# Ordering page loads and page work behind a dense tile's own, and holding the FFN's tiles open over the second out-projection, in a two-layer decoder step

## Chip, cores and metric

One core of one Trainium2 chip runs the whole program. The metric is the device time of one execution in microseconds (us), given as the median of several runs. A profiled execution of the same kernel gives the trace.

## What is computed

The reference runs two layers of a hybrid decoder on 1024 prompt tokens and, with the same weights, on 8 sample tokens that attend to 1024 past tokens in a paged cache. For this case the second part of each layer matters: the sample tokens' attention over the cache, the output projection, and the gated FFN.

```python
# sample tokens: pages of the cache, softmax over past and new keys, difference of two maps
k_past = cache_k[l, page_table].reshape(DB, -1, DIFF_HEADS, 2, DIFF_DK)
v_past = cache_v[l, page_table].reshape(DB, -1, DIFF_HEADS, DIFF_DV)
od = diff_attn_sample(q, k, v, k_past, v_past, lam)
og, s_new = gla_chunk(state_gla[l].astype(jnp.float32), gq, gk, gv, glog)
# both groups of tokens
def merge(o_diff, o_gla, gate, subln_l, gla_norm_l, lam_init, w_out_l):
    od = rmsnorm(o_diff, subln_l) * (1.0 - lam_init)
    og = rmsnorm(o_gla, gla_norm_l).reshape(B, T, GLA_HEADS * GLA_DV) * jax.nn.silu(gate)
    o = jnp.concatenate([od.reshape(B, T, DIFF_HEADS * DIFF_DV), og], axis=-1)
    return o @ w_out_l
def ffn(h, norm2_l, w_gu_l, w_down_l):
    n = rmsnorm(h, norm2_l)
    a, b = jnp.split(n @ w_gu_l, 2, axis=-1)
    return (jax.nn.silu(a) * b) @ w_down_l
```

Everything is float32, D_MODEL is 1024 and D_FF is 2816.

## The kernel before

A layer has three stages. The first two (`phase_d` and `phase_g`) make the input projection, the prompt's attention and the gated linear attention. The third, which the change is about, is the dense stage with the cache work of the sample tokens beside it.

**Dense stage.** The tokens are split in two halves: half 0 has 512 columns, half 1 has 512 and the 8 sample tokens. A half runs `out_half` (out-projection, 8 weight tiles) and then `ffn_half`. The FFN's 22 blocks of 128 come in chunks of 4, the last of 2. A chunk has `gates` (4 weight tiles), `ups` (4) and `down` (8 tiles of 4 blocks each, 2 in the last chunk). The order is gates(0), then for each chunk ups(c), gates(c+1), down(c). Half 0 works in pairs of tiles that share one accumulation group `psd`.

Each weight tile goes through `prep_tile`: SyncE (SP) loads `raw` (3 buffers), ScalarE rounds it to `wh` (3 buffers), VectorE subtracts to get the rest `wl` (2 buffers), each in pieces of 4 blocks (128x512). `gemm3` then issues three matmuls for every block: `wh` with the activations' high part, `wh` with their low part, `wl` with the high part. So SP, ScalarE and VectorE all work ahead of TensorE, by at most 3, 3 and 2 tiles.

`out_half` reads two inputs: `oHa`, `oLa` (attention, loaded from scratch memory by SP) and `oHb`, `oLb` (split on ScalarE and VectorE from `og`, which is on chip), and contracts the a part first. After a group the residual is added, and `new_x` makes the new `xH` and `xL`.

**Cache work.** `decode` reads 64 pages of keys and 64 pages of values (256 KB each, 5 buffers of tag `page`). A key page is multiplied with the query on GpSimd (`page<-page,qbd`) and reduced on VectorE (`sall<-page`). Then comes a softmax, and each value page is weighted either on ScalarE and added on GpSimd, or weighted and added on VectorE (`vacc`). `sample_gla` does the sample tokens' linear attention on GpSimd. All of this runs beside half 0; half 1 needs its result `osf`.

**What sets the order.** A clock written into the code: `dense(us)` and `mix(us)` set the priority of what is traced next to a place on a common clock and move on, by 5.6 us for a gate or up tile and by 1.8 or 1.6 us for a key or value page, times `MIX_RATE` 1.4. The scheduler takes, on each engine, the instruction of the smallest clock value among those that it holds for ready. Each engine then runs its list in order, SP's queue of loads too. `load_page` reads the page's number and issues the load, with an order kept only to the fourth page load before.

**Memory.** Tile pools are stacked; the pool `op` of the second out-projection stands where the pool `fp` of the first FFN half stood, and so waits until that has been read for the last time.

Of the kernel before, what the change touches and what calls it, by code (L numbers as in the profile page):

```python
# [21 lines left out]
P = 128  # L22
# [4 lines left out]
NB = 8  # L27
# [7 lines left out]
MIX_RATE = 1.4  # L35
# [8 lines left out]
NPB = 5  # L44
# [13 lines left out]
def f(ap):  # L58
    return ap.bitcast(F32)
# [3 lines left out]
def hybrid_kernel(  # L63
# [26 lines left out]
    clock = {"base": 0, "top": 0, "dense": 0.0, "mix": 0.0, "rate": 1.0}  # L90

    def span_start():
        clock.update(base=tc.cur_priority + 10, top=0, dense=0.0, mix=0.0)

# [8 lines left out]
    def mix(us):  # L103
        at(clock["mix"])
        clock["mix"] += us * clock["rate"]
# [18 lines left out]
    def tt(out, a, b, op, eng=None):  # L124
        (eng or DVE).tensor_tensor(out, a, b, op=op)  # L125
# [129 lines left out]
    def layer(l):  # L255
# [7 lines left out]
        with ExitStack() as octx:  # L263
# [12 lines left out]
            with ExitStack() as pctx:  # L276
# [17 lines left out]

    def load_page(dst, src, idx):
        with ExitStack() as st:
            if len(page_dma) >= 4:
                st.enter_context(tc.issue_after(page_dma[-4].ins))
            r = SP.value_load(pt_sb[0:1, idx:idx + 1], min_val=0, max_val=NPHYS - 1)
        page_dma.append(SP.dma_start(dst, src[bass.ds(r, 1)].rearrange("o p c -> (o p) c")))  # L300
# [581 lines left out]
    def prep_tile(wps, src, nk):  # L882
        raw = wps[0].tile([P, KD, P], F32, name="raw", tag="raw", bufs=3)
        SP.dma_start(raw[:, :nk, :], src.rearrange("(k p) c -> p k c", p=P))
# [56 lines left out]
    def out_half(l, X, og, osf, ac, wps, psD):  # L941
        W = COLS[X]
        acc = ac.tile([P, KD, WM], F32, name="acc", tag="acc")
        with ExitStack() as st:
# [16 lines left out]
            for js in groups(X, list(range(KD))):  # L961
                ps = psD.tile([P, 2, 512], F32, name="psd", tag="d")
                ws = []
                for half in range(2):
                    for u, j in enumerate(js):
# [3 lines left out]
                        gemm3(unit_outs(ps, X, u), *ws[u], ah, al, range(half * H, half * H + H), first=half == 0, last=half == 1)  # L969
# [9 lines left out]
    def ffn_half(l, X, acc, ac, wps, psD, psn):  # L979
# [3 lines left out]
        with ExitStack() as st:  # L983
            fp = st.enter_context(tc.tile_pool(name="fp", bufs=1, reuse_waits="tile"))
            xh = lambda k: xH[:, k, t0:t0 + W]
            xl = lambda k: xL[:, k, t0:t0 + W]
            chunks = [list(range(c, min(c + 4, NF))) for c in range(0, NF, 4)]
            r = rstd[:, t0:t0 + W].unsqueeze(1)

            def gates(c):  # L990
                sa = fp.tile([P, 4, WM], F32, name="sa", tag="sa", bufs=1)
                for fs in groups(X, chunks[c]):
                    ps = psD.tile([P, 2, 512], F32, name="psd", tag="d")
                    for u, ff in enumerate(fs):
                        dense(5.6)
                        ws = prep_tile(wps, w_gu[l, :, ff * P:(ff + 1) * P], KD)
                        gemm3(unit_outs(ps, X, u), *ws, xh, xl, range(KD))
                    if fs[0] == 0:
                        rms_half(X, psn)
                    n = len(fs)  # L1000
                    i0 = fs[0] - chunks[c][0]
                    tt(unit_view(sa[:, i0:i0 + n, :W], X, n), unit_ps(ps, X, n),
                       unit_view(bc(r, [P, n, W]), X, n), ALU.mult)
                n = len(chunks[c])
                last_silu.append(act(sa[:, :n, :W], sa[:, :n, :W], AF.Silu))
                if X == 0 or c == len(chunks) - 1:
                    load_ln_exp()
                return sa

            def ups(c, sa):  # L1010
                hs = []
                for fs in groups(X, chunks[c]):
                    ps = psD.tile([P, 2, 512], F32, name="psd", tag="d")
                    for u, ff in enumerate(fs):
                        dense(5.6)
                        ws = prep_tile(wps, w_gu[l, :, DFF + ff * P:DFF + (ff + 1) * P], KD)
                        gemm3(unit_outs(ps, X, u), *ws, xh, xl, range(KD))
                    n = len(fs)
                    i0 = fs[0] - chunks[c][0]
                    g = 2 if X == 0 else 1  # L1020
                    tb = fp.tile([P, g, W], F32, name="tb", tag="tb", bufs=1)[:, :n, :]
                    tt(unit_view(tb, X, n), unit_ps(ps, X, n), unit_view(bc(r, [P, n, W]), X, n), ALU.mult)
                    tt(tb, tb, sa[:, i0:i0 + n, :W], ALU.mult)
                    hh = fp.tile([P, g, W], F32R, name="hh", tag="hh", bufs=6 // g)[:, :n, :]
# [283 lines left out]
```

## Time and profile before

| What | Value |
|---|---|
| Median of 3 runs | 2929.18 us (2924.52 to 2933.24) |
| Profiled execution | 2921.56 us, its span 2919.8 us |
| TensorE matmul busy | 2738.3 us (94%) |
| VectorE busy | 1801.9 us (62%) |
| ScalarE busy | 1359.9 us (47%) |
| GpSimd busy | 386.8 us (13%) |
[...]
| SP's queue of loads | 290.90 MB, 33.9% of 16 DMA engines |

The dense stage of the first layer runs from about 534 us to 1460 us of the span, that of the second from about 1975 us to the end, half 0 first (to about 1020 and 2463 us). Busy shares are means over stages with different limits; what an edit in one stage is worth has to be read there. A line such as "[5.14 <-DVE wl]" gives the idle time of an engine ahead of an instruction, and what ended it.

### The profile page before, as it was taken

What the parts mean: (1) busy time and instruction counts of PE and PEld (TensorE: products, weight loads), DVE (VectorE), ACT (ScalarE), POOL (GpSimd) and SP (SyncE); (2) the same over time, 40 slices, a digit from 0 to 9 for tenths busy, and PEclk for the clock granted to TensorE, in tenths of its full rate; (3) what the DMA queues carried; (4) which work ended last, traced back from release to release, by engine and by line L of the source; (5) the groups of instructions that cost most, each with busy time, mean ns of one, the idle gap of its engine ahead of it and who ended that gap; (6) DMA issues with size and microseconds to landing.
All of it is one profiled execution on the core that took longest, in us unless ns stands there. A gap on an engine that the chain in (4) does not pass through costs nothing.

```text
span 2919.8 us, 46807 instructions
## 1 busy us (share of the span) xinstructions
PE 2738.3 (94%) x16906; PEld 2420.4 (83%) x16906; DVE 1801.9 (62%) x3549; ACT 1359.9 (47%) x3343; POOL 386.8 (13%) x333
## 2 busy tenths in 40 slices
PE   8999899969999899999999989999699997999999
PEld 7887787757778699999988868887577885999998
DVE  6777577567775564444577766675778743544444
ACT  7888445423543343222378874454235432322222
POOL 1000000076230000000010000000943300000000
PEclk9999999989999999999999999999799998999999
DMA  4121111267673252332221111113767624223322
GB/s 129 58 58 38 46 31 44 86 198 224 203 205 105 76 151 84 97 95 87 66 50 57 40 33 55 49 45 115 218 187 220 186 81 134 87 88 94 94 85 83
DMA packets 461322, 298.13 MB, mean 102 GB/s; under 512 B 34698, under 2 KB 416906, under 8 KB 461090
## 3 DMA queue, kind: packets, MB, share of 16 engines
q1 hardware_dynamic: 452322, 290.90, 33.9%
q10 hardware_dynamic: 8704, 4.20, 0.5%
q8 instruction: 134, 2.20, 0.3%
q14 instruction: 98, 0.80, 0.1%
q0 software_dynamic: 64, 0.03, 0.0%
HBM read 271.53 MB, written 23.53 MB: 101 GB/s over the span
## 4 chain that ended last, share of the span: by engine, by line
PE 73%; DVE 10%; ACT 8%; DMA 3%; issue 3%; POOL 2%; SPq 1%; DVEq 0%; ACTq 0%; POOLq 0%
PE psd L82 52%; PE psq L82 4%; PE psqk L82 3%; PE psv L82 3%; PE psgg L82 2%; PE po L82 2%; ACT sc L88 2%; ACT qn L88 1%; PE psS L82 1%; POOL page L125 1%; ACT qhh L88 1%; DVE wl L125 1%; PE tpw L85 1%; PE poG L82 1%; DVE gA L720 1%
## 5 line engine op out<-in xcount | busy, mean ns | idle before, releaser
L88 ACT ACTIVATE wh<-raw 128x512 fp32r<-128x512 f32 (+1 forms) x608 | 353.1, 614 | 946.6 <-PE psd L82 753.1
L82 PE MATMUL psd<-xH,wh 128*128 128x260 f32 (+1 forms) x2112 | 681.5, 323 | 39.3 <-ACT wh L88 39.3
L82 PE MATMUL psd<-xH,wl 128*128 128x260 f32 (+1 forms) x2112 | 683.4, 324 | 14.1 <-DVE wl L125 14.0
L82 PE MATMUL psd<-xL,wh 128*128 128x260 f32 (+1 forms) x2112 | 679.1, 322 | 0.6 <-DVE xL L128 0.6
L125 DVE TENSOR_TENSOR wl<-raw,wh 128x512 fp32r<-128x512 f32 (+1 forms) x608 | 444.5, 748 | 108.0 <-issue 57.6
L82 PEld LDWEIGHTS psd<-xH,wh 128*128 128x128 f32 x2112 | 400.0, 189 | 71.1 <-ACT wh L88 40.2
L82 PEld LDWEIGHTS psd<-xH,wl 128*128 128x128 f32 x2112 | 400.2, 190 | 50.8 <-DVE wl L125 18.8
L82 PEld LDWEIGHTS psd<-xL,wh 128*128 128x128 f32 x2112 | 400.3, 190 | 33.8 <-DVE xL L128 1.8
L82 PE MATMUL psd<-hh,wl 128*128 128x260 f32 (+1 forms) x1056 | 341.8, 324 | 12.9 <-DVE wl L125 12.8
L82 PE MATMUL psd<-hh,wh 128*128 128x260 f32 (+1 forms) x1056 | 341.4, 324 | 9.9 <-ACT hh L88 8.6
L82 PE MATMUL psd<-hl,wh 128*128 128x260 f32 (+1 forms) x1056 | 339.8, 322 | 0.3 <-DVE hl L125 0.2
L125 DVE TENSOR_TENSOR acc<-psd,acc 128x520 f32<-128x520 f32 (+1 forms) x144 | 125.7, 873 | 169.6 <-PE psd L82 169.6
L82 PEld LDWEIGHTS psd<-hh,wl 128*128 128x128 f32 x1056 | 200.6, 190 | 33.4 <-DVE wl L125 19.0
L82 PEld LDWEIGHTS psd<-hh,wh 128*128 128x128 f32 x1056 | 200.6, 190 | 25.9 <-ACT hh L88 9.7
L82 PEld LDWEIGHTS psd<-hl,wh 128*128 128x128 f32 x1056 | 200.5, 190 | 16.1 <-DVE hl L125 2.0
L125 POOL TENSOR_TENSOR page<-page,qbd 128x512 f32<-128x512 f32 x128 | 185.9, 1484 | 45.6 <-DMA page<-in_cache_k 37.1
L82 PE MATMUL psq<-wh,xH 128*128 128x384 f32 (+1 forms) x512 | 180.4, 352 | 7.6 <-DVE zs L125 4.7
L82 PE MATMUL psq<-wh,xL 128*128 128x384 f32 (+1 forms) x512 | 179.9, 352 | 0.0
L82 PE MATMUL psq<-wl,xH 128*128 128x384 f32 (+1 forms) x512 | 179.3, 350 | 0.0
L125 DVE TENSOR_TENSOR sa<-psd,rstd 128x520 f32<-128x520 f32 (+1 forms) x66 | 57.6, 873 | 184.7 <-PE psd L82 180.6
L125 DVE TENSOR_TENSOR tb<-psd,rstd 128x520 f32<-128x520 f32 (+1 forms) x66 | 57.6, 872 | 152.2 <-PE psd L82 152.2
L128 DVE SCALAR_TENSOR_TENSOR wl<-raw,g1c,wh 128x256 fp32r<-128x256 f32 (+2 forms) x160 | 81.0, 536 | 96.1 <-ACT wh L88 60.2
(330 smaller groups left out, 5409.4 us busy)
## 6 DMA issues: line engine op xcount, KB each, us to landing
raw<-in_w_gu SPq DMA_DIRECT2D x176, 512.0 KB
raw<-in_w_down SPq DMA_DIRECT2D x160, 256.0 KB
page<-in_cache_k SPq DMA_DIRECT2D x128, 256.0 KB
page<-in_cache_v SPq DMA_DIRECT2D x128, 256.0 KB
raw<-in_w_out SPq DMA_DIRECT2D x32, 512.0 KB
raw<-in_w_in SPq DMA_DIRECT2D x64, 192.0 KB
raw<-in_w_in SPq DMA_DIRECT2D x64, 128.0 KB
xt<-in_x_prompt SPq DMA_DIRECT2D x8, 512.0 KB
```

The source lines that it names most:

```text
L82: PE.matmul(out, lhsT=lhsT, rhs=rhs, start=start, stop=stop, skip_group_check=True)
L85: PE.matmul(out, lhsT=in_, rhs=ident[:n, :n], is_transpose=True)
L88: return ACT.activation(out, in_, func, **kw)
L125: (eng or DVE).tensor_tensor(out, a, b, op=op)
L128: (eng or DVE).scalar_tensor_tensor(out=out, in0=in0, scalar=scalar, in1=in1, op0=op0, op1=op1)
L720: DVE.copy_predicated(av, mv, ps.rearrange("p c e (n m) -> p (c e) n m", m=m))
```

## The change

It has five parts.

1. Page loads, reductions and value work get an order behind a tile of the dense stage: `prep_tile` records its load, its last `wh` and its last `wl` with the clock value (`marks`); `behind(slot, ahead)` orders what is traced in its scope after the mark at the same place of the clock (`ahead` tiles earlier). These are orders on one engine, with no semaphore.
2. The pace: every page takes 2.1 us of the clock (before 2.52 for keys, 2.24 for values), the cache work starts at 58 us of the clock (before 0), and there are 6 page buffers (before 5).
3. The first half's `fp` pool stays open while the second out-projection's pools are laid above it, and the second half's `fp` pool is opened only after that.
4. `out_half` contracts the b part (on chip) ahead of the a part (loaded).
5. `ffn_half` does the last chunk's ups ahead of the down step of the chunk before it.

```diff
-MIX_RATE = 1.4
+MIX_START = 58.0
...
-NPB = 5
+NPB = 6
...
     def mix(us):
         at(clock["mix"])
-        clock["mix"] += us * clock["rate"]
+        clock["mix"] += us
+
+    marks = []
+
+    def mark_at(us, ahead=0):
+        i = max([0] + [n for n, m in enumerate(marks) if m[0] <= us])
+        return marks[max(0, i - ahead)]
+
+    def behind(slot, ahead=0):
+        return tc.issue_after(mark_at(clock["mix"], ahead)[slot].ins)
...
-                with ExitStack() as actx:
-                    ac = new_acc(actx)
-                    acc = out_half(l, 0, og0, osf, ac, wps, psD)
-                    oga.close()
-                    ffn_half(l, 0, acc, ac, wps, psD, psn)
-                    clock["rate"] = MIX_RATE
-                    decode(l, actx, osf, smc, gsm, psX)
-                with ExitStack() as actx:
+                with ExitStack() as fctx:
+                    with ExitStack() as actx:
+                        ac = new_acc(actx)
+                        acc = out_half(l, 0, og0, osf, ac, wps, psD)
+                        oga.close()
+                        ffn_half(l, 0, acc, ac, wps, psD, psn, fctx)
+                        clock["mix"] = MIX_START
+                        decode(l, actx, osf, smc, gsm, psX)
+                    actx = pctx.enter_context(ExitStack())
                     ac = new_acc(actx)
                     acc = out_half(l, 1, og1, osf, ac, wps, psD)
-                    ffn_half(l, 1, acc, ac, wps, psD, psn)
+                ffn_half(l, 1, acc, ac, wps, psD, psn, actx)
...
             if len(page_dma) >= 4:
                 st.enter_context(tc.issue_after(page_dma[-4].ins))
+            st.enter_context(behind(1))
...
-            act(wh[:, ks, :], raw[:, ks, :], AF.Copy)
-            tt(wl[:, ks, :], raw[:, ks, :], f(wh[:, ks, :]), ALU.subtract)
+            rh = act(wh[:, ks, :], raw[:, ks, :], AF.Copy)
+            rl = tt(wl[:, ks, :], raw[:, ks, :], f(wh[:, ks, :]), ALU.subtract)
+        marks.append((clock["dense"], ld, rh, rl))
...
-                        gemm3(unit_outs(ps, X, u), *ws[u], ah, al, range(half * H, half * H + H), first=half == 0, last=half == 1)
+                        gemm3(unit_outs(ps, X, u), *ws[u], ah, al, range((1 - half) * H, (1 - half) * H + H), first=half == 0, last=half == 1)
...
-            for c in range(len(chunks)):
-                hs = ups(c, sa)
-                if c + 1 < len(chunks):
-                    sa = gates(c + 1)
-                down(c, hs)
+        end = len(chunks) - 1
+        for c in range(end):
+            hs = ups(c, sa)
+            sa = gates(c + 1)
+            if c + 1 == end:
+                he = ups(end, sa)
+            down(c, hs)
+        down(end, he)
...
-                mix(1.8)
+                mix(2.1)
                 pg = page(cache_k[l], b, j)
                 tt(pg, pg, qb, ALU.mult, POOL)
-                DVE.tensor_reduce(out=sall[:, j, b, :], in_=pg.rearrange("p (h d) -> p h d", d=DK), axis=AX.X, op=ALU.add)
+                with behind(3, 1):
+                    DVE.tensor_reduce(out=sall[:, j, b, :], in_=pg.rearrange("p (h d) -> p h d", d=DK), axis=AX.X, op=ALU.add)
...
-                mix(1.6)
+                mix(2.1)
```

The value pages' work on ScalarE and on VectorE is put into `behind(2, 1)` and `behind(3, 1)` in the same way.

How the scheduler then writes the lists is seen at three places. The first is VectorE at the start of the cache work, in the first chunk's ups. Before, from the seventeenth reduction of a key page on (`sall`; `tb`, `hl` are the pair's evacuation, `wl` a piece of the next weight tile):

```order
L1094 TENSOR_REDUCE sall<-page 128x8
L125 TENSOR_TENSOR hl<-tb,hh 128x1024
L1094 TENSOR_REDUCE sall<-page 128x8 x2
L125 TENSOR_TENSOR wl<-raw,wh 128x512
L1094 TENSOR_REDUCE sall<-page 128x8 x3
L125 TENSOR_TENSOR tb<-psd,rstd 128x1024
L1094 TENSOR_REDUCE sall<-page 128x8
L125 TENSOR_TENSOR tb<-tb,sa 128x1024
L1094 TENSOR_REDUCE sall<-page 128x8 x2
L125 TENSOR_TENSOR hl<-tb,hh 128x1024
L1094 TENSOR_REDUCE sall<-page 128x8 x11
L125 TENSOR_TENSOR wl<-raw,wh 128x512 x2
```

The change, from the eleventh reduction on:

```order
L1110 TENSOR_REDUCE sall<-page 128x8 x5
L135 TENSOR_TENSOR tb<-psd,rstd 128x1024
L135 TENSOR_TENSOR wl<-raw,wh 128x512
L135 TENSOR_TENSOR tb<-tb,sa 128x1024
L135 TENSOR_TENSOR wl<-raw,wh 128x512
L1110 TENSOR_REDUCE sall<-page 128x8
L135 TENSOR_TENSOR hl<-tb,hh 128x1024
L1110 TENSOR_REDUCE sall<-page 128x8
L135 TENSOR_TENSOR wl<-raw,wh 128x512 x2
L1110 TENSOR_REDUCE sall<-page 128x8 x3
L135 TENSOR_TENSOR tb<-psd,rstd 128x1024
L135 TENSOR_TENSOR wl<-raw,wh 128x512
```

Before, 11 reductions in a row stand ahead of the next tile's two pieces; now at most 5 stand together there, and the pieces stand between the steps of the evacuation.

The second place is SP's queue at the change of halves (`raw` are weight tiles, `oHa` and `oLa` the loaded input of the second out-projection). Before:

```order
L884 DMA raw<-in_w_down 128x4x128 x8
L884 DMA raw<-in_w_gu 128x8x128 x6
L884 DMA raw<-in_w_down 128x4x128 x8
L884 DMA raw<-in_w_gu 128x8x128 x2
L884 DMA raw<-in_w_down 128x2x128 x8
L884 DMA raw<-in_w_out 128x8x128 x3
L950 DMA oHa<-scr_oh_108 128x4x512
L950 DMA oLa<-scr_ol_112 128x4x512
L884 DMA raw<-in_w_out 128x8x128 x2
L212 DMA raw<-in_w_in 128x3x128 x7
```

The change:

```order
L896 DMA raw<-in_w_gu 128x8x128 x6
L963 DMA oHa<-scr_oh_108 128x4x512
L963 DMA oLa<-scr_ol_112 128x4x512
L896 DMA raw<-in_w_down 128x4x128 x8
L896 DMA raw<-in_w_down 128x2x128 x8
L896 DMA raw<-in_w_out 128x8x128 x8
L896 DMA raw<-in_w_gu 128x8x128 x4
```

The two loads have moved from behind the third out-projection tile to ahead of the last 16 down tiles.

The third place is VectorE at the end of half 0 (`acc<-psd` closes a pair of down tiles). Before:

```order
L125 TENSOR_TENSOR wl<-raw,wh 128x512 x3
L125 TENSOR_TENSOR acc<-psd,acc 128x2x512
L125 TENSOR_TENSOR wl<-raw,wh 128x512 x2
L125 TENSOR_TENSOR wl<-raw,wh 128x256
L125 TENSOR_TENSOR tb<-psd,rstd 128x1024
L125 TENSOR_TENSOR wl<-raw,wh 128x256
L125 TENSOR_TENSOR tb<-tb,sa 128x1024
L125 TENSOR_TENSOR hl<-tb,hh 128x1024
L125 TENSOR_TENSOR wl<-raw,wh 128x256
L125 TENSOR_TENSOR acc<-psd,acc 128x2x512
```

The change:

```order
L135 TENSOR_TENSOR sa<-psd,rstd 128x2x512
L135 TENSOR_TENSOR wl<-raw,wh 128x512 x3
L135 TENSOR_TENSOR tb<-psd,rstd 128x1024
L135 TENSOR_TENSOR wl<-raw,wh 128x512
L135 TENSOR_TENSOR tb<-tb,sa 128x1024
L135 TENSOR_TENSOR wl<-raw,wh 128x512
L135 TENSOR_TENSOR hl<-tb,hh 128x1024
L135 TENSOR_TENSOR acc<-psd,acc 128x2x512
L135 TENSOR_TENSOR wl<-raw,wh 128x512 x2
L135 TENSOR_TENSOR acc<-psd,acc 128x2x512
L135 TENSOR_TENSOR wl<-raw,wh 128x512 x2
```

The evacuation of the last ups (`tb`, `tb`, `hl`) stood directly ahead of the down step that reads it; now the down step of the chunk before stands between.

## Rows read from the trace of the kernel before

**Rows 1.** The page of the profile: span, busy time, and a group (busy, mean ns).
```profile
span 2919.8 us, 46807 instructions
...
PE 2738.3 (94%) x16906; PEld 2420.4 (83%) x16906; DVE 1801.9 (62%) x3549; ACT 1359.9 (47%) x3343; POOL 386.8 (13%) x333
...
L88 ACT ACTIVATE wh<-raw 128x512 fp32r<-128x512 f32 (+1 forms) x608 | 353.1, 614 | 946.6 <-PE psd L82 753.1
```

**Rows 2.** Waits on TensorE, whole span: total us, times, longest us.
```profile
PE psd L82 <- ACT wh L88: 44.8, 5, 20.1
...
PE psd L82 <- DMA oHa<-scr_oh: 17.7, 2, 11.6
```

**Rows 3.** Timeline of weight loads, first layer, decode's start: start, us, [idle before <-releaser].
```profile
619.80 0.28 PEld L82 LDWEIGHTS psd<-xH,wl 128*128 128x128 f32 x1 [5.14 <-DVE wl L125]
...
661.70 0.29 PEld L82 LDWEIGHTS psd<-xH,wh 128*128 128x128 f32 x1 [20.57 <-ACT wh L88]
```

**Rows 4.** Windows of tile psd: PE, PEld, DVE, ACT busy (x), granted clock, DMA share.
```profile
610.00:670.00 60.00, 32.70 (x120) 24.92 (x120) 3.64 (x3) 0.00 (x0) 0.77 0.73 221
670.00:690.00 20.00, 20.00 (x88) 16.21 (x87) 2.44 (x2) 0.00 (x0) 1.00 0.62 188
2050.00:2110.00 60.00, 34.89 (x122) 26.64 (x121) 3.65 (x3) 0.00 (x0) 0.74 0.73 218
```

**Rows 5.** Timeline of SyncE's queue, first layer, decode's start.
```profile
611.27 14.06 SPq L300 DMA_DIRECT2D page<-in_cache_k  x11
...
651.82 3.77 SPq L300 DMA_DIRECT2D page<-in_cache_k  x4
655.69 0.40 SPq L884 DMA_DIRECT2D raw<-in_w_gu  x1
```

**Rows 6.** Timeline of GpSimd (first row) and VectorE (second), same place.
```profile
609.22 51.23 POOL L125 TENSOR_TENSOR page<-page,qbd 128x512 f32<-128x512 f32 x36 [2.67 <-DMA qbd<-scr_q]
...
618.61 1.14 DVE L125 TENSOR_TENSOR wl<-raw,wh 128x512 fp32r<-128x512 f32 x1
```

**Rows 7.** Timeline of weight loads at the half change, first layer, then second.
```profile
1001.83 0.50 PEld L82 LDWEIGHTS psd<-hh,wh 128*128 128x128 f32 x2 [4.31 <-ACT hh L88]
...
1026.03 0.29 PEld L82 LDWEIGHTS psd<-oHa,wh 128*128 128x128 f32 x1 [6.55 <-ACT nsq L88]
1028.21 0.29 PEld L82 LDWEIGHTS psd<-oHa,wh 128*128 128x128 f32 x1 [1.89 <-ACT wh L88]
...
2461.11 1.57 PEld L85 LDWEIGHTS psy<-ident,acc 128*128 128x128 f32 x8 [2.96 <-issue]
2474.64 0.50 PEld L82 LDWEIGHTS psd<-oHa,wh 128*128 128x128 f32 x2 [11.96 <-DMA oHa<-scr_oh]
2477.22 0.29 PEld L82 LDWEIGHTS psd<-oLa,wh 128*128 128x128 f32 x1 [2.08 <-DMA oLa<-scr_ol]
```

**Rows 8.** Windows over stretches at half clock: PE busy comes first, clock third last.
```profile
617.90:624.70 6.80, 4.90 (x12) 3.84 (x13) 6.18 (x9) 5.18 (x5) 6.80 (x6) 0.50 0.66 192
1000.20:1007.00 6.80, 5.13 (x11) 3.64 (x12) 2.14 (x3) 1.47 (x2) 0.00 (x0) 0.50 0.07 19
1020.70:1034.30 13.60, 6.65 (x28) 6.30 (x29) 10.52 (x14) 7.85 (x16) 4.53 (x4) 0.50 0.79 255
```

**Rows 9.** VectorE's groups, 662 to 745 us (pages in work): busy us, mean ns.
```profile
L125 DVE TENSOR_TENSOR wl<-raw,wh 128x512 fp32r<-128x512 f32 x30 | 31.8, 1081 | 1.5 <-ACT wh L88 1.2 <-PE psd L82 0.3
L1094 DVE TENSOR_REDUCE sall<-page 128x8 f32<-128x512 f32 x28 | 18.6, 679 | 11.7 <-POOL page L125 11.7
...
L125 DVE TENSOR_TENSOR hl<-tb,hh 128x1024 fp32r<-128x1024 f32 x2 | 3.5, 1770 | 0.5 <-ACT hh L88 0.5
...
L125 DVE TENSOR_TENSOR tb<-psd,rstd 128x1024 f32<-128x1024 f32 x2 | 2.4, 1218 | 0.7 <-PE psd L82 0.7
```

**Rows 10.** VectorE's wl, 905 to 990 us (no pages); then its min/median/max, 590 to 740.
```profile
L125 DVE TENSOR_TENSOR wl<-raw,wh 128x512 fp32r<-128x512 f32 x31 | 20.8, 686 | 14.2 <-issue 10.6 <-PE psd L82 2.3 <-ACT sa L88 1.0
...
L125 DVE TENSOR_TENSOR wl<-raw,wh x42: 671/1134/1782, 591.9 to 739.7; 128x512 fp32r<-128x512 f32 x42
```

More of the change, by code (lines that the diff above doesn't have):

```diff
@@ L977, in out_half, with ffn_half @@
         return acc
-    def ffn_half(l, X, acc, ac, wps, psD, psn):
+    def ffn_half(l, X, acc, ac, wps, psD, psn, st):
         W = COLS[X]
@@ new lines, in ffn_half, with gates @@
+        fp = st.enter_context(tc.tile_pool(name="fp", bufs=1, reuse_waits="tile"))
+        xh = lambda k: xH[:, k, t0:t0 + W]
+        xl = lambda k: xL[:, k, t0:t0 + W]
+        chunks = [list(range(c, min(c + 4, NF))) for c in range(0, NF, 4)]
+        r = rstd[:, t0:t0 + W].unsqueeze(1)
+        def gates(c):
+            sa = fp.tile([P, 4, WM], F32, name="sa", tag="sa", bufs=1)
+            for fs in groups(X, chunks[c]):
+                ps = psD.tile([P, 2, 512], F32, name="psd", tag="d")
+                for u, ff in enumerate(fs):
+                    dense(5.6)
+                    ws = prep_tile(wps, w_gu[l, :, ff * P:(ff + 1) * P], KD)
+                    gemm3(unit_outs(ps, X, u), *ws, xh, xl, range(KD))
+                if fs[0] == 0:
+                    rms_half(X, psn)
+                n = len(fs)
+                i0 = fs[0] - chunks[c][0]
+                tt(unit_view(sa[:, i0:i0 + n, :W], X, n), unit_ps(ps, X, n),
+                   unit_view(bc(r, [P, n, W]), X, n), ALU.mult)
+            n = len(chunks[c])
+            last_silu.append(act(sa[:, :n, :W], sa[:, :n, :W], AF.Silu))
+            if X == 0 or c == len(chunks) - 1:
+                load_ln_exp()
+            return sa
@@ new lines, in down @@
+        def down(c, hs):
+            fs = chunks[c]
+            end = c == len(chunks) - 1
+            if end and last:
+                yall = fp.tile([P, 4, WM], F32, name="yall", tag="sa", bufs=1)
+                ysall = fp.tile([P, 2 if X == 0 else 1, W], F32, name="ysall", tag="tb", bufs=1)
+            for js in groups(X, list(range(KD))):
+                ps = psD.tile([P, 2, 512], F32, name="psd", tag="d")
+                for u, j in enumerate(js):
+                    dense(0.7 * len(fs))
+                    ws = prep_tile(wps, w_down[l, fs[0] * P:(fs[-1] + 1) * P, j * P:(j + 1) * P], len(fs))
+                    gemm3(unit_outs(ps, X, u), *ws, lambda k: hs[k][0], lambda k: hs[k][1], range(len(fs)))
+                n = len(js)
+                av = unit_view(acc[:, js[0]:js[0] + n, :W], X, n)
+                tt(av, unit_ps(ps, X, n), av, ALU.add)
+                if not end:
+                    continue
+                for j in js:
+                    if not last:
+                        new_x(acc, ac, X, j, eng=POOL)
+                        continue
+                    psy = psn.tile([P, 512], F32, name="psy", tag="n").rearrange("p (i t) -> p i t", t=P)
+                    for i in range(4):
+                        pe_t(psy[:, i, :], acc[:, j, i * P:(i + 1) * P], P)
+                    yt = yall[:, j % 4, :HALF].rearrange("p (i t) -> p i t", t=P)
+                    act(yt, psy, AF.Copy)
+                    SP.dma_start(y_prompt[t0:t0 + HALF, j * P:(j + 1) * P].rearrange("(i t) c -> t i c", t=P), yt)
+                    if X:
+                        pss = psn.tile([P, 512], F32, name="psys", tag="n")
+                        pe_t(pss[0:NB, 0:P], acc[:, j, HALF:WM], P)
+                        ys = ysall[0:NB, 0, (j % 4) * P:(j % 4 + 1) * P]
+                        DVE.tensor_copy(ys, pss[0:NB, 0:P])
+                        SP.dma_start(y_sample[:, j * P:(j + 1) * P], ys)
@@ L1189, in decode_v @@
                     for h in range(H):
-                        if first[0]:
-                            DVE.tensor_scalar(out=acc[:, h, :], in0=p4[:, h, :], scalar1=w4[:, h:h + 1], scalar2=None, op0=ALU.mult)
-                        else:
-                            stt(acc[:, h, :], p4[:, h, :], w4[:, h:h + 1], acc[:, h, :], ALU.mult, ALU.add)
+                        with behind(3, 1):
+                            if first[0]:
+                                DVE.tensor_scalar(out=acc[:, h, :], in0=p4[:, h, :], scalar1=w4[:, h:h + 1], scalar2=None, op0=ALU.mult)
+                            else:
+                                stt(acc[:, h, :], p4[:, h, :], w4[:, h:h + 1], acc[:, h, :], ALU.mult, ALU.add)
                 first[int(on_pool)] = False
```

113 lines of the change are left out of this document (29 added, 84 removed).

## Prediction

> **What bounds the kernel now.** I read the page first: TensorE's matmuls are busy for 2738.3 of 2919.8 us [rows 1], so an order alone can win only what TensorE loses, which is idle time and time at the lower clock. Next I read TensorE's waits over the whole span: the longest single wait is 20.1 us for ScalarE's `wh`, and two waits for the loaded `oHa` take 17.7 us [rows 2]. Then I looked up where these stand. Nearly all of it lies at two places of each layer: the start of the cache work, and the change from half 0 to half 1.
>
> At the start of the cache work the weight loads wait 5.14 us for a `wl`, and later 20.57 us for a `wh` [rows 3]. To size the loss with its clock, count matmuls: undisturbed, 88 are done in 20 us at full clock, 4.4 per us. In the 60 us from 610 us on there are 120, which would take 27.3 us; 32.7 us are lost. In the second layer 122 are done in such a stretch, so 32.3 us are lost [rows 4]. The cause stands in SP's queue: from 611.27 us on it issues 11, then twice 8, then 4 page loads (31), and only then, at 655.69 us, the next weight tile [rows 5]. Each of these waits for a page buffer, so for GpSimd, which takes 51.23 us for 36 products, 1.42 us each [rows 6]. The pages stand first because the clock puts the cache work at 0, while it begins some 75 us later; it is behind its pace, and everything that it is behind goes ahead of the weights. The earlier wait is another: on VectorE 7 reductions, each as slow as GpSimd's products, stand ahead of the piece of `wl` that starts at 618.61 us [rows 6], and the matmul that needs it starts at 619.80 us [rows 3].
>
> At the change of halves the first layer waits 4.31 us for `hh` of the last ups, 6.55 us until `oHa` has landed and its tile is rounded, and 1.89 us for a `wh`. The second layer has the same 4.31 us, then 2.96 us ahead of the transposes of the output, 11.96 us for `oHa` and 2.08 us for `oLa` [rows 7]. [...]
>
> **The change, part by part.** *Order and pace (parts 1 and 2).* With the cache work at 58 us of the clock little is behind its pace, and the list of SP now has 9 page loads at most between two weight tiles, where it had 31. Nine pages at 1.42 us are 13 us, less than the three tiles of 24 matmuls (5.45 us each at 4.4 per us) by which SP may be ahead. So the 20.57 us wait should go. The first wait stays: still 7 reductions stand ahead of that `wl`. I keep its 5.1 us whole, and half of the 4.90 us that TensorE then works at half clock [rows 8], 2.5 us: 7.6 us a layer. Its other end is 2.5 us less, if GpSimd starts earlier by the 2.67 us that it waits for the query [rows 6], whose load now stands ahead of a store. What returns: 32.7 + 32.3 - 2 x 7.6 = **49.8 us**.
>
> What is late next is VectorE. Pages that were reduced while TensorE stood still now run beside running tiles. For one pair of tiles, 48 matmuls, TensorE needs 10.9 us; the clock gives a pair 11.2 us, so 5.33 pages. With the pages in work VectorE needs 1.081 us for each of four `wl`, 0.679 for a reduction, 1.22 for `tb` and for the other operations of 1024 columns, 1.77 for `hl` [rows 9]. A pair of ups is then 4.32 + 2 x 1.22 + 1.77 + 3.62 = 12.15 us, 1.25 over TensorE's time. A pair of gates is 4.32 + 1.22 + 3.62 = 9.2 us, 1.7 under; a pair of down tiles 2.16 + 1.22 + 1.81 = 5.2 of 5.45 us. Four ups pairs fall among a layer's key pages: 5 us if nothing is recovered, 10 us in both layers; none if the gates' room takes it up. I take the middle, **5 us** lost. The value pages need less per page on VectorE and run at nearly the rate they had; I cost them at nothing beyond waits of this size, which are in the trace already. The sixth buffer and the orders themselves cost nothing, as they add no instruction to an engine.
>
> [...] First the rows: with pages in work a `wl` takes 1.081 us on the mean [rows 9], without 0.686, and at most 1.782 [rows 10]. [...]
>
> *The second out-projection's tiles (part 3) and its contraction (part 4).* With space of its own, `oHa` is loaded ahead of the last 16 down tiles and `oHb` is split during the last gates and ups, so neither is waited for: 6.55 + 1.89 us in the first layer, 11.96 + 2.08 in the second [rows 7]. In the second, 12 matmuls of the new half also stand in TensorE's list ahead of the last transposes, which covers the 2.96 us. *The last ups earlier (part 5)* covers the 4.31 us in each layer: 8 down tiles stand between the evacuation and its reader. With the clock this is 12.75 + 5.9 and 21.3 + 5.9, together **45.9 us**. Against it stands what is late next: the new half's first `wl` is queued on VectorE behind one closing of a group (1.22 us) and one product like `wl`, so 1.22 + 2 x 0.686 = 2.6 us a layer [rows 9, 10]. And with the b part first, the first matmul of `out_half` needs the second piece of a tile's `wh`: at the start of half 0 one more `wh`, 0.6 us [rows 1], a layer. Together 6.4 us; at least nothing, where tiles are ahead. Half 1 is otherwise the same work.
>
> The sum: 49.8 - 5 + 45.9 - 6.4 = 84.3 us. The profiled execution took 2921.56 us, so **2837 us**. The median before was 7.6 us above its profiled execution, and the range takes that in.
>
> **Rivals.** *The half change gives nothing.* The two loads now stand in SP's queue ahead of 16 weight tiles, and they need the space of the cache work's pools, so they wait for its last GpSimd operation. By the clock it ends at 58 + 128 x 2.1 + 34 for the steps between = 361 us; the last 16 down tiles begin at 380, and SP, three tiles of 5.6 us ahead, comes to the loads at 363. If the cache work is late by more than the three tiles that are loaded, TensorE waits there instead: 39.5 us less, 2876 us. For it: the margin is one page. Against: late pages hold the weights in the same list too, so both clocks slip together.
>
> *Every `wl` is blocked.* At 1.782 us a `wl` [rows 10], a pair of ups is 4.05 us over, a pair of gates 1.07, a pair of down tiles 1.15; over a layer's key pages (4, 4 and 8 pairs) that is 16.2 + 4.3 + 9.2 = 29.7 us, 59 in both in place of 5: 2891 us. For it: GpSimd now works beside running tiles all the time. Against: 1.081 is a mean over such a stretch.
>
> *Slower: the pages set the pace.* Weight loads and pages now stand in one fixed list. In the 83 us from 662 us on 28 pages were reduced [rows 9], 2.96 us each, where the new order asks for 2.1 x 5.45 / 5.6 = 2.04. If that was a limit and not the old order, 64 key pages take 59 us longer in each layer: 2837 - 5 + 117 = 2949 us. It decides from 2.74 us a page on, where (84.3 + 5) / 128 = 0.70 us more eat the gain. Against: GpSimd does a page in 1.42 us when it is fed [rows 6], VectorE needs 0.679.
>
> *No change*, if SP was held by something that no order moves, such as the landing of the loads. Against: DMA engines were busy for 0.73 of that stretch, and 0.62 right behind it [rows 4].
>
> **How the numbers follow.** About 0.3% (9 us) can be told from no change. The forecast has a chance of 0.70 and reaches from 2806 (all 65.0 + 45.9 us, and 5 us of small waits) to 2860 (VectorE's 10 us, both first waits longer, the median's 7.6). The half change giving nothing 0.11, blocked `wl` 0.09, slower 0.05, no change 0.05. The range of 2806 to 2880 holds the forecast, the first of the rivals and part of the second, a little over 8 in 10. Faster takes the first three and a little of the last, 0.91; same 0.03; slower 0.06.
>
> **What would show it.** Right: no stretch without matmuls in ups of the first chunk apart from one of 3 to 5 us for `wl`; some 230 matmuls in the 60 us behind the first page product (52.4 us at 4.4); no wait for `oHa`; the first `hh` of the last down tile without a wait. Wrong: waits for `wl` that repeat in every pair of ups, with a mean `wl` above 1.3 us; SP standing at `oHa` while `wh` is waited for; weight loads that land late behind pages.

## The result, and the profile after

The changed kernel takes 2843.2 us, median of 4 runs (2836.4 to 2846.1), against 2927.15 us of the kernel before on the same chip: a ratio of 0.9707, 95% interval 0.9683 to 0.9731. Timed again, beside one of the experiments, it took 2838.15 us (5 runs, 2837.2 to 2840.3): 0.9697, 0.9681 to 0.9712. The forecast was 2837 us in a range of 2806 to 2880. The medians differ by 84.0 us and by 90.0 us, where 84.3 was forecast. The first profiled execution took 2846.1 us; its span is 75.5 us below that of before [rows 1], and the rest of this section accounts for those 75.5.

From the page of the changed kernel:

```profile
span 2844.3 us, 46804 instructions
...
PE 2723.1 (96%) x16906; PEld 2406.7 (85%) x16906; DVE 1804.5 (63%) x3549; ACT 1361.1 (48%) x3343; POOL 386.3 (14%) x333
```

Busy times are those of [rows 1] but for TensorE's, which is 15 us less, as more of its work is done at full clock (mean granted clock 0.985, before 0.971). TensorE's waits over the whole span:

```profile
PE psd L82 <- DVE wl L135: 35.5, 28, 5.0
...
PE psd L82 <- ACT wh L88: 7.5, 4, 2.5
```

The waits for `wh` have fallen from 44.8 to 7.5 us, those for `oHa` are gone [rows 2]. What is left are waits for `wl`. The timeline of TensorE's weight loads at the first layer's decode start:

```profile
624.67 0.29 PEld L82 LDWEIGHTS psd<-xH,wl 128*128 128x128 f32 x1 [5.41 <-DVE wl L135]
...
641.63 0.19 PEld L82 LDWEIGHTS psd<-xH,wl 128*128 128x128 f32 x1 [1.30 <-DVE wl L135]
645.56 0.19 PEld L82 LDWEIGHTS psd<-xH,wl 128*128 128x128 f32 x1 [1.31 <-DVE wl L135]
...
683.15 0.19 PEld L82 LDWEIGHTS psd<-hh,wl 128*128 128x128 f32 x1 [4.52 <-DVE wl L135]
```

The first of these was kept in the sum (5.1 us), the 20.57 us for `wh` [rows 3] does not come back, and a new wait of 4.52 us stands in the first down step. Windows of tile `psd` over the 60 us behind the first page product, in both layers (columns as in [rows 4]):

```profile
614.00:674.00 60.00, 53.28 (x220) 41.99 (x219) 6.87 (x6) 0.00 (x0) 0.94 0.61 187
2021.00:2081.00 60.00, 53.54 (x221) 42.09 (x220) 7.30 (x6) 0.00 (x0) 0.97 0.61 188
```

220 and 221 matmuls, where 120 and 122 were done before [rows 4]. At 4.4 per us, 10 us are lost there. The forecast kept 7.6 us of the start, which it named as some 230 matmuls, and 2.5 us a layer for the pages' spread. In SP's queue a weight tile stands between every few pages, where 31 pages had stood in a row [rows 5]:

```profile
616.15 11.10 SPq L312 DMA_DIRECT2D page<-in_cache_k  x9
627.36 0.40 SPq L896 DMA_DIRECT2D raw<-in_w_gu  x1
628.62 0.33 SPq L312 DMA_DIRECT2D page<-in_cache_k  x1
...
671.65 0.35 SPq L1104 DMA_DIRECT2D qbd<-scr_q  x1
672.10 1.51 SPq L1125 DMA_DIRECT2D S<-in_state_gla  x2
```

The last row is where the 4.52 us come from. These two loads of the sample tokens' state stood in the queue behind a load of the query that SP issued at 671.65 us, when GpSimd had ended, at 671.62, the last product with the query whose buffer it takes. GpSimd waited for one (first row below), it could not go on with the pages until then, and on VectorE the reduction of a page stands ahead of the `wl` that TensorE waits for (GpSimd's timeline, then VectorE's):

```profile
676.59 1.04 POOL L135 TENSOR_TENSOR S<-S,smc 128x512 f32<-128x512 f32 x1 [4.96 <-DMA S<-in_state_gla]
```

```profile
681.36 0.69 DVE L1110 TENSOR_REDUCE sall<-page 128x8 f32<-128x512 f32 x1 [6.34 <-POOL page L135]
681.97 1.13 DVE L135 TENSOR_TENSOR wl<-raw,wh 128x512 fp32r<-128x512 f32 x1
```

The second layer has the same wait in the same step (timeline of weight loads):

```profile
2089.76 0.29 PEld L82 LDWEIGHTS psd<-hh,wl 128*128 128x128 f32 x1 [4.62 <-DVE wl L135]
```

At the half change the timeline of weight loads has, first layer and then second, against [rows 7]:

```profile
990.19 0.19 PEld L82 LDWEIGHTS psd<-hh,wl 128*128 128x128 f32 x1 [1.12 <-DVE wl L135]
...
992.23 0.19 PEld L82 LDWEIGHTS psd<-hh,wl 128*128 128x128 f32 x1 [1.27 <-DVE wl L135]
...
995.39 0.19 PEld L82 LDWEIGHTS psd<-hh,wl 128*128 128x128 f32 x1 [1.93 <-DVE wl L135]
...
998.78 0.29 PEld L82 LDWEIGHTS psd<-oHb,wh 128*128 128x128 f32 x1 [2.63 <-ACT wh L88]
...
2405.63 0.19 PEld L82 LDWEIGHTS psd<-oHb,wh 128*128 128x128 f32 x1 [0.77 <-ACT wh L88]
```

No 4.31 us for `hh`, no `oHa`. The second layer is nearly free of waits. In the first, VectorE holds the last `wl` pieces behind `new_x`, which the next layer needs (its timeline):

```profile
990.06 1.78 DVE L135 TENSOR_TENSOR xL<-acc,xH 128x512 fp32r<-128x512 f32 x1
991.76 0.41 DVE L135 TENSOR_TENSOR wl<-raw,wh 128x256 fp32r<-128x256 f32 x1
```

This `xL` of `new_x` takes 1.78 us, where the one at 986.34 us takes 0.69. GpSimd was at work on the norm's sum of squares when it began, and it ends 0.55 us behind GpSimd's operation (GpSimd's timeline):

```profile
989.99 1.30 POOL L135 TENSOR_TENSOR ssq<-ssq,nsq 128x512 f32<-128x512 f32 x1 [0.74 <-ACT nsq L88]
```

The last section shows the same for `wl`. The granted clock is at 0.50 here again, for 6.8 us (window of the whole core, clock third last):

```profile
997.40:1004.20 6.80, 4.22 (x18) 3.92 (x19) 6.80 (x7) 5.54 (x10) 4.53 (x4) 0.50 0.40 120
```

Cut by stage (from a stage's first weight load to that of the next, in the timelines), the difference of the two profiled executions is, in us:

| Stage | layer 0: before, after | difference, forecast | layer 1: before, after | difference, forecast |
|---|---|---|---|---|
| out-projection of half 0 | 47.7, 50.5 | +2.8, +0.6 | 47.4, 50.0 | +2.6, +0.6 |
| first gates and ups | 100.8, 77.8 | -23.0, -22.6 | 100.5, 77.4 | -23.0, -22.2 |
| first down step | 23.4, 30.1 | +6.7, 0 | 23.2, 29.2 | +6.0, 0 |
| middle chunks | 221.6, 214.0 | -7.6, 0 | 221.3, 218.4 | -2.9, 0 |
| last gates, ups and downs | 95.3, 87.4 | -7.9 | 104.0, 84.3 | -19.7 |
| half 1 and what follows | 952.2, 947.6 | -4.6 | 445.1, 438.6 | -6.5 |
| last two rows together | | -12.5, -16.0 | | -26.2, -24.6 |

With 1.9 us more ahead of the first row (a stage that the change doesn't touch) the differences make -75.5 before rounding. The forecast's 2.5 us a layer for the pages' spread are counted in the second row, though two of their four pairs of ups stand in the middle chunks.

### The profile page after: what moved, and what is told of

Read it like the earlier page. It is cut to its first block, busy times and chain, and to the rows that moved or that the text cites. A ratio compares the mean times of both kernels' runs of the same rounds, so it can differ in the third digit from the quotient of the medians.

```text
span 2844.3 us, 46804 instructions
## 1 busy us (share of the span) xinstructions
PE 2723.1 (96%) x16906; PEld 2406.7 (85%) x16906; DVE 1804.5 (63%) x3549; ACT 1361.1 (48%) x3343; POOL 386.3 (14%) x333
## 4 chain that ended last, share of the span: by engine, by line
PE 72%; DVE 12%; ACT 8%; issue 3%; DMA 3%; POOL 2%; SPq 0%; DVEq 0%; ACTq 0%; POOLq 0%
PE psd L82 51%; PE psq L82 4%; PE psv L82 3%; PE psqk L82 3%; DVE wl L135 2%; PE psgg L82 2%; PE po L82 2%; ACT sc L88 2%; POOL page L135 1%; ACT qn L88 1%; ACT qhh L88 1%; PE poG L82 1%; PE psS L82 1%; PE tpw L85 1%; DMA page<-in_cache_k 1%
## 5 line engine op out<-in xcount | busy, mean ns | idle before, releaser
L135 DVE TENSOR_TENSOR wl<-raw,wh 128x512 fp32r<-128x512 f32 (+1 forms) x608 | 454.2, 764 | 90.3 <-issue 51.4
```

The source lines that it names most:

```text
L135: return (eng or DVE).tensor_tensor(out, a, b, op=op)
```

## The experiments

Each is an edit of the changed kernel. Two profiled executions of the changed kernel itself have spans of 2844.3 and 2838.0 us, and half 0 of its second layer takes 459.3 and 453.0 us in them; a difference of that size between single executions says nothing. So I read stages, which repeat better, and lean on a span only where it is clear of that. The experiments ran on four chips. The kernel before took 2919.4 to 2934.4 us beside them, and 2922.0 to 2934.5 us in nine runs on one of the chips, so a single run can't tell the chips apart.

**The orders alone taken away** (part 1; pace, start and buffers stay):

```diff
-            st.enter_context(behind(1))
...
-                with behind(3, 1):
+                if True:
```

(and in the same way the two scopes of the value pages.)

> The changed kernel without its orders behind the dense tiles; pace, start at 58 us, six buffers and parts 3 to 5 stay. Theory (the place on the clock removed the burst of page loads, the orders only tidy): the 20 us wait at the start of the cache work stays away, the span is within 10 us of the changed kernel's 2844.3 us, say 2836 to 2856. Rival (the orders removed it): the wait of about 20 us is back in each layer, 2880 to 2890 us.

Span 2872.9 us, 17 us above the theory's range and 7 below the rival's, though the 20 us wait stays away. The waits are many and small:

```profile
PE psd L82 <- DVE wl L135: 47.0, 36, 5.3
PE psd L82 <- ACT wh L88: 13.2, 6, 2.9
```

The first gates and ups take 77.4 us in both layers, as with the orders. The middle chunks take 228.0 and 230.9 us in place of 214.0 and 218.4, since mainly their down steps wait for `wl` and `wh`. So part 2 alone frees the decode start: SP's longest row of page loads is 9 here too. The orders are worth about 13 us a layer in the middle, more than I had thought.

**The old pace and start, with the orders** (part 2):

```diff
-MIX_START = 58.0
+MIX_START = 0.0
-NPB = 6
+NPB = 5
```

(and 1.8 and 1.6 us times 1.4 a page.)

> The changed kernel with the old pace (2.52 and 2.24 us a page, start at 0, five buffers); orders and parts 3 to 5 stay. Theory: 31 page loads stand ahead of one weight tile again, a wait near 20 us in each layer, gates and ups before the first down step take 100 us where they take 77.7; with the first down step quick again, span 2880 to 2890 us. Rival (the orders are what counts): under 2856 us, no wait over 6 us there.

Span 2877.8 us, 2 us under the expected range. SP's queue has 11, 8, 8 and 4 page loads, 31 in all, ahead of one weight tile again. The timeline of weight loads has the old wait back, in the same place:

```profile
666.48 0.29 PEld L82 LDWEIGHTS psd<-xH,wh 128*128 128x128 f32 x1 [20.54 <-ACT wh L88]
```

The first gates and ups take 102.3 us. The orders don't mend a start that is behind its clock. In the code, the mark that a page looks up by an early clock value is that of an early tile, which has long been loaded. The start, the time per page and the number of buffers were undone together; which of the three counts was not tried.

**Both undone** (parts 1 and 2):

> Parts 1 and 2 both undone, parts 3 to 5 stay, so the start of the cache work is the old one and the half change the new one. Half 0 (first psd matmul to that of half 1) took 488.8 and 496.4 us before, 459.7 and 459.3 after; either of parts 1 and 2 alone missing gave 474 to 477. Theory (the two overlap: the pace removes the one long wait, the orders only work under the new pace, because under the old one the scheduler puts the dense work ahead by itself): about as without the pace, halves of 473 to 480 us, span 2875 to 2885. Rival (both add up): halves of 488 or more, span 2900 or more.

Span 2897.8 us, 53.5 above the changed kernel, with halves of 489.6 and 483.1 us: over the theory's 473 to 480, and one of the two under the rival's 488. One part alone costs 28.6 and 33.5, together 62.1. They nearly add, nearer to the rival: part 2 works at the decode start and the orders behind it, two places and not one.

**The `fp` pool closed as before** (part 3):

```diff
-                    actx = pctx.enter_context(ExitStack())
-                    ac = new_acc(actx)
-                    acc = out_half(l, 1, og1, osf, ac, wps, psD)
+                actx = pctx.enter_context(ExitStack())
+                ac = new_acc(actx)
+                acc = out_half(l, 1, og1, osf, ac, wps, psD)
```

> Part 3 undone: the first FFN half's pool is closed before the second out-projection's pools are laid, which then wait for its last reader. Theory: the wait for the loaded part and for the splits is back at the half change, partly covered by the part that is contracted first; half 0 plus half 1 of the first layer 5 to 11 us longer, the second layer's 12 to 18: 2861 to 2873 us. Rival (the order of contraction alone covers it): within 5 us of 2844.3.

Span 2856.7 us, 12.4 above the changed kernel: 4 us under the theory's range and 7 above the rival's. The last down steps and half 1's out-projection together take 94.3 and 94.4 us in place of 88.8 and 83.9: 16 us. In the weight loads' timeline the wait at the half change of the first layer is

```profile
1003.55 0.29 PEld L82 LDWEIGHTS psd<-oHb,wh 128*128 128x128 f32 x1 [6.93 <-ACT wh L88]
```

In the second layer TensorE waits 3.15 us there for the split `oHb` and 2.89 us for the loaded `oHa`, so both waits that part 3 was to remove are back.

**The last ups at their old place** (part 5):

```diff
-            if c + 1 == end:
-                he = ups(end, sa)
...
-        down(end, he)
+        down(end, ups(end, sa))
```

> The changed kernel with the last chunk's ups in their old place behind the down step. Theory: 4.3 us for the rounded hh and 0.8 for its rest come back at the end of half 0 in each layer, with about 2.6 us at half clock, and 2 us at the end of the second layer: 2857 to 2863 us. Rival (that wait would be hidden by what the other parts freed): within 3 us of 2844.3.

Span 2866.4 us, of which 4 us stand ahead of the dense stage. The 4.31 us are back, to the hundredth [rows 7]:

```profile
989.13 0.50 PEld L82 LDWEIGHTS psd<-hh,wh 128*128 128x128 f32 x2 [4.31 <-ACT hh L88]
```

From the last gates to the end of half 1's out-projection it takes 7.2 and 6.9 us more. That is the wait, 0.76 us for `hl` behind it, and about 2 us of clock in each layer, where TensorE's granted clock is at 0.50 for 6.8 us more than in the changed kernel (in the first layer the weight loads behind the wait begin 0.43 us apart up to 994.40 us, and 0.23 us apart from 995.08 us on). The theory's mechanism holds, and the rest of its excess lies outside these stages.

**The loaded part contracted first, as before** (part 4):

```diff
-                        gemm3(unit_outs(ps, X, u), *ws[u], ah, al, range((1 - half) * H, (1 - half) * H + H), first=half == 0, last=half == 1)
+                        gemm3(unit_outs(ps, X, u), *ws[u], ah, al, range(half * H, half * H + H), first=half == 0, last=half == 1)
```

> The changed kernel with the loaded part of the out-projection contracted first again. Theory: half 0's out-projection falls from 50.5 to about 47.6 us in each layer, as before the change, because the first matmul of a tile needs the first piece of its rounded weights and not the second; half 1 does not change, its loads landed some 60 us early; 2837 to 2841 us. Rival (the order of contraction is needed for the half change): waits for the loaded part of 6 to 12 us at the half change, 2852 us or more.

Span 2833.8 us, 3 us under the expected range. Nothing waits for the loads at the half change; the waits there are 1.13 us for `wh` and 2.39 for `wl`, in place of 2.63 and 1.50. The last down steps and half 1's out-projection take as long as in the changed kernel, and half 0's out-projection takes 47.8 us, not 50.5. So part 4 has a cost, and returns nothing once part 3 is there. Timed, with the changed kernel on the same chip:

> The changed kernel itself, timed again beside the next kernel on the same chip: a ratio to the kernel before of 0.968 to 0.974, as in its first timing (0.971).

> The changed kernel without part 4 (the loaded part of the second out-projection is contracted first), timed. Theory (part 4 costs about 2.7 us of waits at each half 0 and what TensorE then loses on its clock, and saves nothing at the half change, where the operand has long landed): 4 to 12 us less than the changed kernel on the same chip, ratio to the kernel before 0.965 to 0.969. Rival (the 10 us between the two profiled executions are chance, as executions of the changed kernel lie up to 10 us apart): within 3 us of it.

2834.9 us (5 runs, 2830.2 to 2838.2), ratio 0.9688 (0.9673 to 0.9704), against 2838.15 us and 0.9697 (0.9681 to 0.9712). The stages say the same again: out-projection of half 0 47.6 and 47.4 us against 50.5 and 49.2; the last downs with the next out-projection 88.9 and 83.6 against 88.7 and 83.6. The cost is shown in its stage, about 2.5 us a layer. The times differ by 3.3 us, below the theory's 4 to 12, and their intervals overlap, so a gain of the whole program is not shown.

**The state's loads behind the dense tile too**, for the starvation that is left:

```diff
+                    with behind(1):
+                        SP.dma_start(S0[64 * e:64 * e + 64], state_gla[l, bs, h].rearrange("b d v -> d b v"))
+                        SP.dma_start(vb[64 * e:64 * e + 64],
+                                     scr_gv[l][bs, h * DV:(h + 1) * DV].unsqueeze(0).to_broadcast([64, 4, DV]))
```

> The changed kernel, with the loads of the sample tokens' linear attention also ordered behind the dense tile at their place of the clock (they ran at the start of the cache work and again in its middle, in the first down steps). Theory: the two longest waits that are left, 5.1 to 5.4 us at the start and 4.5 us in the first down step, stand behind GpSimd work of that attention and SP's waits for its store; both go, with some of the half clock behind each: 9 us of waits and 2 to 3 us of clock in each layer, 2820 to 2828 us. Rival (VectorE is short of time there, whatever GpSimd does first): both waits stay above 3 us, 2838 us or more.

Span 2838.3 us. The start wait falls from 5.41 to 3.30 us and the 4.52 us wait to 2.83, yet half 0 takes 458.8 us in place of 459.7 in the first layer, and 453.6 in the second, where the two executions of the changed kernel took 459.3 and 453.0. The span is the rival's, and so is one of the two waits. In the first layer the stages up to the end of the first down step are 5.2 us shorter and the middle chunks 4.4 longer, with new waits of 1 to 2 us. With part 4 undone as well:

> The run before it, with the loaded part contracted first, which alone gave 2833.8 us of span against 2844.3. Theory: the two add up, 2810 to 2818 us. Rival (the contraction's gain came from the start of the cache work, by chance of the schedule): no more than 3 us under the run before it.

Span 2838.2 us, half 0 459.6 and 453.4 us. The two don't add, and the span is that of the run before it, as the rival had it. The waits only move.

**GpSimd's product on the key pages left out.**

```diff
-                tt(pg, pg, qb, ALU.mult, POOL)
```

> The changed kernel without GpSimd's product on the key pages: VectorE reduces the raw page (this leaves out the product of the keys with the query). Theory (what is left of the starvation at the decode starts comes from these products: they slow VectorE's weight-load copies to a mean of 1.21 us where 0.68 was seen with nothing beside them, and they hold the reductions that stand ahead of a copy): the 5.41 us start wait falls below 1 us, the 4.52 us wait of the first down step below 2 us, the mean copy in 618 to 745 to about 0.7 us, and each half 0 (459.7 and 459.3 us) is shorter by 12 us or more; span 2815 to 2822 us against 2844.3. Rival (SP's row of loads and VectorE's own work set the waits): the copies get shorter, but the waits move to other places and each half 0 gains less than 6 us; span 2832 us or more.

Span 2808.9 us, 35 us less and 6 us under the theory's range, half 0 443.3 and 439.9 us: the theory's way, and more of it. VectorE's groups from 618 to 745 us, in the changed kernel and then here:

```profile
L135 DVE TENSOR_TENSOR wl<-raw,wh 128x512 fp32r<-128x512 f32 x40 | 47.6, 1209 | 0.0
L1110 DVE TENSOR_REDUCE sall<-page 128x8 f32<-128x512 f32 x59 | 38.5, 676 | 14.8 <-POOL page L135 14.8
...
L135 DVE TENSOR_TENSOR tb<-tb,sa 128x1024 f32<-128x1024 f32 x4 | 7.0, 1760 | 0.0
```

```profile
L1109 DVE TENSOR_REDUCE sall<-page 128x8 f32<-128x512 f32 x50 | 32.8, 679 | 7.7 <-DMA page<-in_cache_k 7.7
L135 DVE TENSOR_TENSOR wl<-raw,wh 128x512 fp32r<-128x512 f32 x43 | 30.2, 722 | 8.0 <-issue 8.0
...
L135 DVE TENSOR_TENSOR tb<-tb,sa 128x1024 f32<-128x1024 f32 x4 | 4.9, 1217 | 0.0
```

A `wl` costs 0.722 us in place of 1.209, `tb<-tb,sa` 1.217 in place of 1.760; the reduction costs the same, 0.679 and 0.676. The windows have 254 and 256 matmuls, where 60 us at 4.4 per us would be 264:

```profile
614.00:674.00 60.00, 59.04 (x254) 47.24 (x253) 8.55 (x7) 0.00 (x0) 1.00 0.75 221
2021.00:2081.00 60.00, 59.41 (x256) 47.67 (x255) 8.55 (x7) 0.00 (x0) 1.00 0.83 246
```

The first down step is back at 23.5 and 23.1 us. So what is left at the decode start is GpSimd's product: what it does to VectorE's operations, and the reductions that wait for it ahead of a `wl`. The run takes both away and does not tell their shares.

**Key pages slower, value pages faster** (2.35 and 1.85 us of the clock, the same total, with part 4 undone):

```diff
-                mix(2.1)
+                mix(2.35)
...
-                mix(2.1)
+                mix(1.85)
```

> The changed kernel with the loaded part of the second out-projection contracted first (as in e4_a_first), and the key pages every 2.35 us of the clock, the value pages every 1.85 us (together as long as 2.1 us each). Theory (VectorE is short of time in the stretch of the key pages and has some left beside the value pages, whose copies took a mean of 0.80 us): the waits of the key stretch fall, those of the value pages grow by less, and each half 0 is shorter by 3 to 8 us than in e4_a_first (456.5 and 453.2 us); span 2818 to 2828 us against 2833.8. Rival (the total of VectorE's work in half 0 counts, and waits only move): each half 0 within 2.5 us of e4_a_first; span 2830 to 2840 us.

Span 2853.7 us: neither, it is slower by 20 us than the kernel that it edits. The longest wait of the first down step falls (from 4.41 to 3.27 us in the first layer, from 4.68 to 3.20 in the second), but the step is no shorter: 30.3 and 29.5 us, where it took 29.5 and 29.6. One wait of TensorE, for GpSimd's sum of the value pages, is new:

```profile
PE psov L82 <- POOL vacc L135: 9.2, 2, 4.6
```

In the second layer TensorE's granted clock is at 0.50 for 41 us of half 0, where it was for 16. So at 1.85 us a value page the sum comes late for its place in TensorE's list. In single runs 2.1 and 2.1 was better than this split, and no other split was tried.

## Why the prediction held, step by step

- **Decode start, 49.8 us less 5 of the pages.** Right, in its place and size: 23.0 us a layer were won in the first gates and ups, where the terms give 22.6 and 22.2. Part 2 undone alone brings the 20.5 us wait back, so part 2 is the cause; which of start, pace and buffers is not shown. The sum has no term for the orders by themselves: they hold the middle chunks, where they are worth 13 us a layer.
- **What the pages cost.** The step that failed is "a pair of down tiles 2.16 + 1.22 + 1.81 = 5.2 of 5.45 us", a cost of nothing: the first down step takes 6.7 and 6.0 us more, 4.52 and 4.62 of it in one wait. The mean load of a tile doesn't decide there, but one page that comes late, as VectorE's list has its reduction ahead of a `wl`. The middle chunks, costed at nothing too, gave 7.6 and 2.9 us back.
- **Every `wl` blocked.** I costed VectorE with the mean, 1.081 us, and the rival set every `wl` at the longest, 1.782. The last section shows what the mean is made of: of the `wl` that began beside a GpSimd operation, 29 of 30 ended 0.54 to 0.55 us behind that operation, and they took 0.77 to 1.80 us, by how long it still ran. The trace before held this already: of the 30 `wl` of [rows 9], 12 began with no GpSimd operation running and took 0.68 us, 18 began beside one and took 1.35 on the mean. So the wait that the rival counts on is there, but not in every `wl`, and not always at full length; as a price (59 us) it was too high, as leaving out the whole product gives 35.
- **The half change, 45.9 less 5.2 for its first `wl`.** Measured 38.7 in the last two rows, where 40.7 was forecast: 26.2 in the second layer against 24.6, 12.5 in the first against 16.0. The sum's 5.9 us of clock in each layer are shown as such by no run: they were my estimate, half of the two busy times of TensorE that [rows 8] have at the first layer's half change at a granted clock of 0.50, and taken for the second layer too. There the windows of before from 2440.6 to 2447.5 and from 2461.1 to 2481.6 us have 5.70 and 7.12 us of busy time at 0.51 and 0.50, of which half is 6.4. After the change the first layer has 4.22 us at 0.50, of which half is 2.1, and the second has none (granted clock 1.00 from 2395 to 2425 us). In the first layer the 5.9 us were counted as returned whole, but the three waits behind `new_x` (1.12, 1.27, 1.93 us) stand as before (1.16, 1.27, 1.92), and the new half's first `wh` is waited for 2.63 us. Part 3 and part 5, each undone, cost 16 and 14 us in these stages.
- **Part 4, 0.6 us a layer.** It takes 2.5, and covers nothing that part 3 leaves.
- **Rivals on the range.** The loads of `oHa` were issued at 932 us and first used at 1004.9, and nothing waited for them: the first rival did not come. The pages did not set the pace either: 59 were reduced in the 127 us from 618 us on, 2.15 us each, where 2.74 would have eaten the gain. Between the two profiled executions the sum is 9 us too high. Against it went 12.7 us in the first downs, 4.2 in the out-projections of half 0, 2.0 at the half change and 1.9 ahead of the stage; for it, 10.5 in the middle chunks and 1.3 in the first gates and ups. So part of its closeness is luck: misses of both signs that cancel.

## What to carry to other kernels

When background work is written into fixed lists, give it a start and a pace at which it is truly ready: an order behind a place of the clock did nothing here for work that was already behind its clock, and with the new start and pace the orders were worth 13 us a layer in the stages behind the start. After each such repair look at which operations still stand ahead of the critical one on its engine and whom they wait for: here only leaving out GpSimd's product, which the result needs, won clearly, and shifting single waits brought the next ones in. A slow mean of an operation should be split into its cases before it is used as a price: here 1.209 us was 0.68 for 10 of 40, and up to 1.80 for the others.

## What the hardware showed that was not expected

**A `wl` that began beside a GpSimd operation ended 0.55 us behind it.** The mean of 1.209 us hides two cases. From 618 to 745 us, 10 of the 40 `wl` began with no GpSimd operation running, and took 0.68 us each. Of the 30 others, 29 ended 0.54 to 0.55 us after the GpSimd operation that ran when they began, whether that still took 0.22 or 1.25 us; one began together with a product and took 0.68. An example with one of each case, GpSimd's timeline and then VectorE's:

```profile
670.32 1.30 POOL L135 TENSOR_TENSOR page<-page,qbd 128x512 f32<-128x512 f32 x1 [0.59 <-DVE wl L135]
```

```profile
671.40 0.77 DVE L135 TENSOR_TENSOR wl<-raw,wh 128x512 fp32r<-128x512 f32 x1
...
674.34 0.68 DVE L135 TENSOR_TENSOR wl<-raw,wh 128x512 fp32r<-128x512 f32 x1
```

The product ends at 671.62 and the `wl` at 672.17, 0.55 us behind it. At 674.34 GpSimd is waiting for the state (idle until 676.59), and the `wl` takes 0.68. The longest, 1.77 to 1.80 us, began when a product had 1.22 to 1.25 us still to run. It goes the other way too: of the 24 products that began beside a `wl`, 23 ended 1.13 to 1.17 us behind it and took 1.30 to 1.75 us; the other ended 1.75 us behind it and took 1.85. 12 products that began with no VectorE operation running took 1.26 to 1.30 us. The products of 2.27 to 2.28 us began beside a `tb` or an `hl` of 1024 columns.

The reductions show no such wait: they take 676 ns with the product and 679 without it. By what means the one operation holds the other is not shown.

**The clock also fell where TensorE counts as busy.** In the slower-keys kernel, two windows of 7 us behind each other:

```profile
2306.00:2313.00 7.00, 7.00 (x47) 6.49 (x45) 2.22 (x6) 5.97 (x15) 3.43 (x3) 0.90 0.37 115
2313.00:2320.00 7.00, 7.00 (x21) 5.25 (x22) 4.17 (x12) 1.77 (x5) 0.59 (x2) 0.62 0.54 150
```

TensorE is busy for all 7.00 us of both, and of the 7 us ahead of them. Its granted clock is 1.00 in those, 0.90 in the first window and 0.62 in the second; this makes 1.4 and 5.3 us at 0.50, so the fall begins near 2311.6 us (an estimate from these shares). TensorE's work ahead of the fall is narrow (its timeline; `psov` and `pss` are small products of the sample tokens):

```profile
2308.81 0.95 PE L82 MATMUL psov<-ones,vacc 128*128 128x1 f32 x8
2309.61 1.93 PE L82 MATMUL pss<-hsel,vb 128*128 128x2 f32 x16
2311.40 1.73 PE L82 MATMUL psov<-ones,vacc 128*128 128x1 f32 x8
```

These rows, 32 matmuls of one or two columns, follow each other directly. In the changed kernel the clock falls at 2311.5 us, behind 24 of them from 2309.10 us on: it is 1.00 from 2304.7 to 2311.5 us and 0.75 from there to 2318.4, with TensorE busy for all of both. That the narrow work makes the clock fall is not shown: no run takes it away.
